# A hybrid conv / chunked-gMLP decoder layer on one core: first two steps reordered, conv taps moved to a two-way filter, output projection by halves

## The chip, the cores and the metric

One NeuronCore of one Trainium2 chip runs the whole program. The metric is the device time of one execution in microseconds (us); lower is better. TensorE (PE) multiplies, VectorE (DVE), ScalarE (ACT) and GpSimd (POOL) do the rest, SyncE (SP) issues most DMAs.

## The reference, cut to what matters

```python
def _layer(x, conv_buf, chunk_len, norm_g, w_in, conv_w, conv_b, ...):
    h = _rmsnorm(x, norm_g)
    z = h @ w_in                                    # 1024 -> 6144
    a_val, a_gl, a_gate, b_u, b_v, b_gate = jnp.split(z, ...)
    a_in = a_val * jax.nn.sigmoid(a_gl)
    a_seq = jnp.concatenate([conv_buf, a_in], axis=1)
    a_conv = _depthwise_conv_valid(a_seq, conv_w, conv_b)          # 31 taps
    a_out = silu(_layernorm(a_conv, a_ln_g, a_ln_b)) * silu(a_gate)
    vn = _layernorm(b_v, b_ln_g, b_ln_b)
    gated = _spatial_gate(vn in chunks of 128, w_s, b_s)
    b_out = b_u * gated * silu(b_gate)
    y = x + jnp.concatenate([a_out, b_out], axis=-1) @ w_out       # 2048 -> 1024
    return y, new_buf, b_v[:, -chunk_len:]
```

One layer, then a final RMSNorm. 1024 prompt positions and 8 sample positions are computed together (1032 columns), all in float32; channels lie on the 128 partitions.

## The kernel before, in words

**Products.** Every float32 factor is split into a high part h (rounded to fp32r by an ACT copy) and a low part l (DVE: factor minus h), and a product is three matmuls: h·H, l·H, h·L. The input projection is done by Strassen's scheme with 7 products: `PRODS` (line 37) names for each *slot* 0 to 6 of a *step* the weight piece, the form of x (nB11, nT3, T2, nB21, T1, nT4, nB22) and the PSUM bank. `prod` (261) issues 24 matmuls of 258 columns for one slot. A step computes two 128-channel blocks (a *unit*) for all 1032 columns; steps 0 and 1 are special, they compute units P0 and P1 together for the first half of the columns and then for the second half, since x is still being prepared. There are 24 steps (`steps`, 804): `P` units feed the conv, `v` the spatial gate's input, `B` its u and gate, `G` the conv branch's gate.

**Order.** The program is written out by hand, engine queues run in the order in which the code calls them. During steps 0 and 1 `start_x` (846) prepares the forms of x (`xform`, 229: a DVE difference, an ACT copy h, a DVE subtraction l) and the weights' sums and splits (`wsum` 150, `wsplit` 155), after the slot's matmuls. The RMS statistic of the second column half comes from four ACT squares and 96 small matmuls (`stat_q`, 198) in slots 2 and 3 of step 0. PSUM is moved on by ACT copies between banks (lines 944, 948, 952) and read out by `evac0` (ACT) and `evac1` (DVE).

**Fill.** Work without a fixed place stands in a queue `fill`, and `pump` (101) takes from it while the estimated DVE time is below the estimated PE time plus a margin. The conv of channel tile k (`conv_items`, 339) enters it when unit Pk is finished. 20 of its 31 taps are done in pairs on DVE: 10 pairs (`NF`, 337), each three multiply-adds of 512 columns (line 369), the first of them an ACT product. The other 11 taps are ACT products of 1024 columns (`prod`, 379 and 381) that are added up by accumulating DMAs issued from POOL (385), alternately into two buffers; two more accumulating DMAs add these to the result `c` (407), then `c` is added to a running sum `ssum` and stored (331 to 334). After tile 7 come mean, centring (444), squares, variance (`var`), and, once the steps are over, the normalisation `mixa_norm`, `mixa_gate`. All these share a pool of 51 buffers of 4 KB per partition (`U`, tag "u"), where a new tile waits until the buffer's last reader or writer is done.

**Output projection.** `ow` (657) has 48 passes: 3 column groups (384, 384, 264) x 2 halves of the 2048 inputs (the spatial half first, then the conv half) x 8 output tiles. Each pass loads and splits its weights anew (`load_w`, `split_w`) and issues 24 matmuls (`mmo`, 698); both halves of an output tile add up in PSUM. Within the first group's spatial half the layer norm's rest is pumped.

```python
    657	    ow = [(g, half, nt) for g in range(NG) for half in (1, 0) for nt in range(8)]
    382	                if n < 2:
    383	                    st["g", n] = p
    384	                else:
    385	                    G.dma_start(st["g", n % 2], p, accum_op=ALU.add)
    102	        while fill and est["dve"] < est["pe"] + margin:
```

Of the kernel before, what the change touches and what calls it, by code (L numbers as in the profile page):

```python
# [27 lines left out]
EPS = 1e-6  # L28
NU = 51
# [12 lines left out]
def body(ctx, tc, xT, w_in, w_out, state, stateT, conv_w, vecs, wsT, w00, b_s,  # L42
# [36 lines left out]
    cws = C([128, 8, 10], "cws")  # L79
# [75 lines left out]
    def wsplit(u, i):  # L155
        if i == 4:
            t = U([128, 2, 512], f"HL{u}_4", F32R)
            h, l, r = t[:, 0:1, :], t[:, 1:2, :], R[u, 4][:, 0:1, :]
        else:
            h = U([128, 2, 512], f"H{u}_{i}", F32R)  # L160
            l = U([128, 2, 512], f"L{u}_{i}", F32R)
            r = R[u, i]
        HL[u, i] = (h, l)
        A.activation(h, r, AF.Copy)  # L164
        V.tensor_tensor(out=l, in0=r, in1=h, op=ALU.subtract)  # L165
        dve(0.62 if i == 4 else 1.15)

# [22 lines left out]

    def stat_x(p, ps):
# [5 lines left out]

    def stat_q(p, q, ps):
        sq = xsq.pop((p, q))
        for t in range(2):  # L200
            for c in range(6):
                T.matmul(ps[:CN, 0, c:c + 1], lhsT=sq[:, t, c // 3, CN * (c % 3):CN * (c % 3) + CN], rhs=ones_m[:, :1],
                         start=q == 0 and t == 0 and c == 0, stop=q == 3 and t == 1, skip_group_check=True)
# [23 lines left out]
    raw = {}  # L227

    def xform(p, name):
# [3 lines left out]
        if name in ("nB11", "nB21", "nB22"):  # L233
            kh, a = {"nB11": (0, 0), "nB21": (1, 0), "nB22": (1, 1)}[name]
            for j in range(2):
                src = X[p, 2 * kh + j][:, :, a, :]
                hv = h[:, 2 * j:2 * j + 2, :]
                A.activation(hv, src, AF.Copy, scale=-1.0)
                V.scalar_tensor_tensor(out=l[:, 2 * j:2 * j + 2, :], in0=src, scalar=-1.0, in1=hv, op0=ALU.mult,  # L239
                                       op1=ALU.subtract)  # L240
            dve(1.3)
# [13 lines left out]
        V.tensor_tensor(out=l, in0=t, in1=h, op=ALU.subtract)  # L255
        dve(2.4)
# [80 lines left out]
    NF = 10  # L337

    def conv_items(k, ap):
# [26 lines left out]
        def taps(i):  # L366
            def f():
                for e in range(3):
                    V.scalar_tensor_tensor(out=st["m"][e], in0=src(e, i), scalar=wt(e, i), in1=st["m"][e],  # L369
                                           op0=ALU.mult, op1=ALU.add)  # L370
            return f

        def gtap(n):

            def f():
# [6 lines left out]
                if n < 2:  # L382
                    st["g", n] = p
# [736 lines left out]
```

## Time and profile before

| | |
|---|---|
| median of 3 runs | 870.5 us (869.26 to 873.74) |
| the profiled execution | 872.84 us, its span (first to last instruction) 871.1 us |
| PE busy | 777.8 us (89%), 5720 matmuls |
| DVE / ACT busy | 606.4 us (70%) / 435.9 us (50%) |
| mean granted TensorE clock | 0.941 of full speed (2.4 GHz) |

An engine's busy time counts overlapping instructions once. Matmuls are pipelined: one shows some 0.28 us, but in a full stream a new one starts every 0.12 us. "L" numbers are lines of the kernel.

### The profile page before, as it was taken

To read this page: it belongs to the slowest core of one execution; us is meant where nothing else is said; L and a number is where in the kernel's file an instruction comes from. 1 tells how busy PE (TensorE), PEld (TensorE's weight loads), DVE (VectorE), ACT (ScalarE), POOL (GpSimd) and SP (SyncE) were. 2 spreads that over 40 slices of the span, in tenths; PEclk is the share of its full clock that TensorE was granted. 3 is DMA by queue.
4 is the path that set the end of the run, shared out by engine and by line. 5 is a ranking of instruction groups with operands and counts; after the bars stand their busy time and mean duration, and the time that the engine had idled before them with its cause. 6 is when DMAs were issued, how large, how long until landed. Compare 5 with 4: busy or idle time off the path is not lost. (4 is left out here: it accounts for less than half of the span.)

```text
span 871.1 us, 14256 instructions
## 1 busy us (share of the span) xinstructions
PE 777.8 (89%) x5720; PEld 762.3 (88%) x5720; DVE 606.4 (70%) x860; ACT 435.9 (50%) x594; POOL 97.5 (11%) x119
## 2 busy tenths in 40 slices
PE   7797999798887879989799788899999889999995
PEld 6797999798887778989799788899999889999995
DVE  5648998695867568868788787698327756726843
ACT  4443465565545646457574665354336534414431
POOL 1010012121211211211112131000100000000000
PEclk8879999999997989989999899999999999999997
DMA  8031268797895797985979989572369544384461
GB/s 298 0 120 68 75 145 188 179 246 163 202 204 109 225 222 152 215 225 101 249 159 243 213 190 219 199 230 96 112 200 374 168 141 145 115 323 121 133 232 51
DMA packets 68091, 153.56 MB, mean 176 GB/s; under 512 B 7512, under 2 KB 28696, under 8 KB 68008
## 3 DMA queue, kind: packets, MB, share of 16 engines
q1 hardware_dynamic: 53624, 100.15, 33.6%
q0 software_dynamic: 14400, 52.49, 30.9%
q8 instruction: 45, 0.74, 0.4%
q14 instruction: 22, 0.18, 0.1%
HBM read 80.41 MB, written 24.38 MB: 120 GB/s over the span
## 5 line engine op out<-in xcount | busy, mean ns | idle before, releaser
L165 DVE TENSOR_TENSOR L<-R,H 128x1024 fp32r<-128x1024 f32 x72 | 87.9, 1222 | 81.8 <-ACT H L164 60.1
L704 PE MATMUL po<-mh,wh 128*128 128x384 f32 (+1 forms) x384 | 124.5, 324 | 3.9 <-ACT wh L670 3.9
L704 PE MATMUL po<-mh,wl 128*128 128x384 f32 (+1 forms) x384 | 124.3, 324 | 1.9 <-DVE wl L672 1.9
L704 PE MATMUL po<-ml,wh 128*128 128x384 f32 (+1 forms) x384 | 124.0, 323 | 0.2 <-DVE ml L695 0.2
L381 ACT ACTIVATE prod<-apad,cw 128x1024 f32<-128x1024 f32 x80 | 90.7, 1146 | 64.7 <-DMA prod<-prod 40.6
L269 PE MATMUL zb<-hT,H 128*128 128x258 f32 x384 | 84.8, 304 | 25.2 <-ACT zb L944 14.8
L369 DVE SCALAR_TENSOR_TENSOR m<-d,cw,m 128x512 f32<-128x512 f32 x144 | 101.5, 747 | 0.0
L385 POOL DMA_DIRECT2D prod<-prod x72 | 62.4, 866 | 308.5 <-ACT prod L381 198.8
L269 PE MATMUL zb<-hnB,HL 128*128 128x258 f32 x384 | 73.6, 308 | 23.6 <-DVE apad L303 15.7
L164 ACT ACTIVATE H<-R 128x1024 fp32r<-128x1024 f32 x72 | 75.4, 1050 | 34.1 <-DMA prod<-prod 11.9
L269 PEld LDWEIGHTS zb<-hT,H 128*128 128x128 f32 x384 | 64.2, 205 | 27.8 <-ACT zb L944 15.8
L269 PEld LDWEIGHTS zb<-hnB,HL 128*128 128x128 f32 x384 | 60.4, 210 | 26.4 <-DVE apad L303 16.9
L269 PE MATMUL zb<-lT,H 128*128 128x258 f32 x384 | 82.2, 298 | 0.7 <-DVE lT L255 0.7
L269 PE MATMUL zb<-hT,L 128*128 128x258 f32 x384 | 82.3, 297 | 0.0
L269 PE MATMUL za<-lnB,H 128*128 128x258 f32 x384 | 78.0, 285 | 1.4 <-DVE lnB L239 1.4
L269 PE MATMUL za<-hnB,H 128*128 128x258 f32 x384 | 78.3, 285 | 0.0
L269 PE MATMUL za<-hnB,L 128*128 128x258 f32 x384 | 77.9, 284 | 0.0
L704 PEld LDWEIGHTS po<-mh,wh 128*128 128x128 f32 x384 | 73.1, 190 | 4.5 <-ACT wh L670 4.5
L704 PEld LDWEIGHTS po<-mh,wl 128*128 128x128 f32 x384 | 73.3, 191 | 3.0 <-DVE wl L672 2.8
L704 PEld LDWEIGHTS po<-ml,wh 128*128 128x128 f32 x384 | 73.0, 190 | 0.5 <-DVE ml L695 0.5
L672 DVE TENSOR_TENSOR wl<-wr,wh 128x1024 fp32r<-128x1024 f32 x48 | 58.1, 1222 | 17.2 <-ACT wh L670 15.1
L269 PEld LDWEIGHTS zb<-lT,H 128*128 128x128 f32 x384 | 64.4, 205 | 1.0 <-DVE lT L255 1.0
(172 smaller groups left out, 1622.2 us busy)
## 6 DMA issues: line engine op xcount, KB each, us to landing
prod<-prod POOLq DMA_DIRECT2D x72, 512.0 KB, 6.2
R<-w_in SPq DMA_DIRECT2D x96, 256.0 KB, 5.8
wr<-w_out SPq DMA_DIRECT2D x48, 512.0 KB, 4.9
c<-prod POOLq DMA_DIRECT2D x14, 512.0 KB, 4.6
x<-xT SPq DMA_DIRECT2D x8, 516.0 KB, 6.0
mbD<-row SPq DMA_DIRECT2D x8, 516.0 KB, 3.8
vD<-va SPq DMA_DIRECT2D x8, 512.0 KB, 5.8
vh<-vD SPq DMA_DIRECT2D x8, 512.0 KB, 9.1
```

The source lines that it names most:

```text
L164: A.activation(h, r, AF.Copy)
L165: V.tensor_tensor(out=l, in0=r, in1=h, op=ALU.subtract)
L269: T.matmul(z[:, s, :PW], lhsT=HL[u, wi][we][:, wh, cs], rhs=F[name, p][xe][:, kt, :], start=first, stop=(kt == 3 and we == 1), skip_group_ ...
L369: V.scalar_tensor_tensor(out=st["m"][e], in0=src(e, i), scalar=wt(e, i), in1=st["m"][e], op0=ALU.mult, op1=ALU.add)
L381: A.activation(p, ap[:, j:j + NP_], AF.Copy, scale=cw[:, k, j:j + 1])
L385: G.dma_start(st["g", n % 2], p, accum_op=ALU.add)
L672: V.tensor_tensor(out=wl[s], in0=r, in1=wh[s], op=ALU.subtract)
L704: T.matmul(z, lhsT=w[:, cs], rhs=m_[g, half, kt][e], start=(half == 1 and kt == 0 and e == 0 and w is wh[s]), stop=(half == 0 and kt == KT ...
```

## The change

Three parts. (1) In steps 0 and 1 the two halves of `xform` are called apart (`xpre`: difference and h; `xpost`: l), `wsplit` likewise (`whigh`, `wlow`), and `start_x` runs ahead of a slot's matmuls and in a new order; the second half's squares come before the first step and are added up by three accumulating DMAs from POOL, so that 12 small matmuls (24 instructions, each float32 one counting twice) take the place of 96. (2) `NF` is 12: 24 taps go by pairs on DVE, 7 by ACT products, with one accumulating buffer instead of two; the three multiply-adds of a pair are pumped one by one. (3) The output projection does the spatial half for all columns first, 8 passes that are added to x in SBUF (`evac_h`), then the conv half by column groups with 8 weight tiles that stay: 16 splits instead of 48.

```diff
+NF = 12
-    cws = C([128, 8, 10], "cws")
+    cws = C([128, 8, NF], "cws")
...
+    def sum_x_dma(p):
+        for a, b in ((0, 1), (2, 3), (0, 2)):
+            G.dma_start(xsq[p, a], xsq.pop((p, b)), accum_op=ALU.add)
...
-    NF = 10
-
     def conv_items(k, ap):
...
-        def taps(i):
+        def taps(i, e):
             def f():
-                for e in range(3):
-                    V.scalar_tensor_tensor(out=st["m"][e], in0=src(e, i), scalar=wt(e, i), in1=st["m"][e],
-                                           op0=ALU.mult, op1=ALU.add)
+                V.scalar_tensor_tensor(out=st["m"][e], in0=src(e, i), scalar=wt(e, i), in1=st["m"][e],
+                                       op0=ALU.mult, op1=ALU.add)
             return f
...
-                if n < 2:
-                    st["g", n] = p
+                if n == 0:
+                    st["g"] = p
                 else:
-                    G.dma_start(st["g", n % 2], p, accum_op=ALU.add)
+                    G.dma_start(st["g"], p, accum_op=ALU.add)
...
-            while n * (NF - 1) < i * len(others):
+            while n < len(others) and n * (NF - 3) < i * len(others):
                 fill.append(("dve", 0.0, gtap(n)))
                 n += 1
-            fill.append(("dve", 2.0, taps(i)))
+            for e in range(3):
+                fill.append(("dve", 0.665, taps(i, e)))
...
-            for e in range(2):
-                g = st.pop(("g", e))
-                if k < 7:
-                    G.dma_start(c[:, :NP_], g, accum_op=ALU.add)
-                else:
-                    V.tensor_tensor(out=c[:, :NP_], in0=c[:, :NP_], in1=g, op=ALU.add)
+            g = st.pop("g")
+            if k < 7:
+                G.dma_start(c[:, :NP_], g, accum_op=ALU.add)
+            else:
+                V.tensor_tensor(out=c[:, :NP_], in0=c[:, :NP_], in1=g, op=ALU.add)
...
-    ow = [(g, half, nt) for g in range(NG) for half in (1, 0) for nt in range(8)]
+    ow = [(half, nt) for half in (1, 0) for nt in range(8)]
...
+    def evac_h(nt, z, c):
+
+        y = yt[nt]
+        if z is not None:
+            yy = y[:, :768].rearrange("p (a b) -> p a b", a=2)
+            V.tensor_tensor(out=yy, in0=z[:, :, :384], in1=yy, op=ALU.add)
+            dve(0.9)
+        else:
+            V.tensor_tensor(out=y[:, GS[2]], in0=c, in1=y[:, GS[2]], op=ALU.add)
+            dve(0.4)
...
+        for q in range(4):
+            square_x(1, q)
+        sum_x_dma(1)
...
         def start_x(si, slot):
 
             if si == 0:
                 if slot == 0:
-                    xform(0, "T2")
-                    for u in range(2):
-                        wsum(u, "S2")
-                        wsplit(u, 2)
+                    both(lambda u: wsum(u, "S2"), lambda u: whigh(u, 2))
+                    xpost(0, "T2")
+                    xpre(0, "nB21")
+                    both(lambda u: wlow(u, 2))
...
                 if slot == 4:
+                    ps = PS("e", "xst1")
+                    stat_x(1, ps)
+                    rstd_x(1, ps)
+                if slot == 5:
                     bcast_x(1, PS("e", "xbc1"))
...
+        for s in range(8):
+            nt = ow[s][1]
+            z = PS("ab"[nt % 2], f"pz{nt}")
...
+            for g in range(NG):
+                dst = z[:, g, :384] if g < 2 else zc[:, nt % 2, :264]
+                mmo(dst, s, g, range(0, 4))
+                if g == 0:
...
+                    split_w(s + 1)
+                pump(3.0 if nt < 7 else 1e9, nt < 7)
+                mmo(dst, s, g, range(4, 8))
...
+        for g in range(NG):
+            for nt in range(8):
+                s = 8 + nt
...
+                if g == 0:
+                    load_w(s + 2)
+                    split_w(s + 1)
```

What the order looks like on the engines that wait, at three places.

ACT's queue in step 0 before, from the copy for form T2 on (xsq are the second half's squares, H the weights' high parts, hnB, hT, hnT the forms' high parts; p and zc are copies out of PSUM):

```order
L254 ACTIVATE hT_0_303<-tT_0_305 128x1032
L164 ACTIVATE H_2_311<-R_2_147 128x1024
L164 ACTIVATE H_2_316<-R_2_149 128x1024
L948 ACTIVATE p_0_345<-ze_320 128x516
L183 ACTIVATE xsq_0_347<-x_0_151 128x1032
L183 ACTIVATE xsq_1_349<-x_1_153 128x1032
L238 ACTIVATE hnB_0_351<-x_2_130 128x516
L238 ACTIVATE hnB_0_351<-x_3_132 128x516
L183 ACTIVATE xsq_2_357<-x_2_155 128x1032
L183 ACTIVATE xsq_3_359<-x_3_157 128x1032
L952 ACTIVATE zc_386<-zb_301 128x2x258
```

And with the change:

```order
L190 ACTIVATE xsq_3_269<-x_3_157 128x1032
L255 ACTIVATE hnT_0_280<-tnT_0_282 128x1032
L255 ACTIVATE hT_0_286<-tT_0_288 128x1032
L164 ACTIVATE H_2_296<-R_2_147 128x1024
L164 ACTIVATE H_2_299<-R_2_149 128x1024
L242 ACTIVATE hnB_0_303<-x_2_130 128x516
L242 ACTIVATE hnB_0_303<-x_3_132 128x516
L973 ACTIVATE zb_333<-za_293 128x2x258
L255 ACTIVATE hT_0_338<-tT_0_340 128x1032
L164 ACTIVATE H_3_344<-R_3_143 128x1024
L164 ACTIVATE H_3_347<-R_3_145 128x1024
L977 ACTIVATE p_0_374<-ze_335 128x516
```

The squares have moved ahead of hnT; the PSUM copy zb, which slot 2 needs (before it stood ahead of hT), now stands behind both H_2 and hnB.

POOL's queue for conv tile 0, before (the accumulating DMAs of the products, named by tap, into two buffers, then both into c):

```order
L385 DMA prod0_0_976<-prod0_22_1083 128x1024
L385 DMA prod0_21_978<-prod0_23_1123 128x1024
L385 DMA prod0_0_976<-prod0_24_1160 128x1024
L385 DMA prod0_21_978<-prod0_25_1231 128x1024
L385 DMA prod0_0_976<-prod0_26_1234 128x1024
L385 DMA prod0_21_978<-prod0_27_1252 128x1024
L385 DMA prod0_0_976<-prod0_28_1283 128x1024
L385 DMA prod0_21_978<-prod0_29_1330 128x1024
L385 DMA prod0_0_976<-prod0_30_1427 128x1024
L407 DMA c0_1447<-prod0_0_976 128x1024
L407 DMA c0_1447<-prod0_21_978 128x1024
```

And with the change:

```order
L395 DMA prod0_0_937<-prod0_25_970 128x1024
L395 DMA prod0_0_937<-prod0_26_1103 128x1024
L395 DMA prod0_0_937<-prod0_27_1174 128x1024
L795 AFFINE_SELECT wst_787<-wst_787 128x1024
L395 DMA prod0_0_937<-prod0_28_1368 128x1024
L395 DMA prod0_0_937<-prod0_29_1388 128x1024
L395 DMA prod0_0_937<-prod0_30_1459 128x1024
L417 DMA c0_1722<-prod0_0_937 128x1024
```

Eleven DMAs have become seven, and each of the seven now follows its predecessor into or out of the same buffer.

DVE's queue at the end of the last step (23), before (L and HL are the weights' low parts, row is a PSUM read-out, ml the low part of the projection's spatial input, wl of its weights):

```order
L165 TENSOR_TENSOR L_2_6358<-R_2_6213,H_2_6357 128x1024
L165 TENSOR_TENSOR L_3_6415<-R_3_6150,H_3_6414 128x1024
L165 TENSOR_TENSOR HL_4_6458<-R_4_6148,HL_4_6458 128x512
L303 TENSOR_TENSOR row_23_6541<-zb_6411,p_23_6442 128x2x258
L695 TENSOR_TENSOR ml_6545<-mr_0_6444,mh_6544 128x768
L695 TENSOR_TENSOR ml_6549<-mr_1_6447,mh_6548 128x768
L672 TENSOR_TENSOR wl_6554<-wr_6487,wh_6552 128x1024
L303 TENSOR_TENSOR row_23_6541<-zc_6485,p_23_6442 128x2x258
L695 TENSOR_TENSOR ml_6583<-mr_2_6450,mh_6582 128x768
L695 TENSOR_TENSOR ml_6587<-mr_3_6453,mh_6586 128x768
```

And with the change (c7 is the conv result of tile 7, prod7_0 its accumulating buffer, lc a centred tile):

```order
L414 TENSOR_TENSOR c7_6259<-m01_7_5746,m2_7_5747 128x512
L419 TENSOR_TENSOR c7_6259<-c7_6259,prod7_0_5832 128x1024
L168 TENSOR_TENSOR L23_3_6266<-R23_3_5958,H23_3_6265 128x1024
L168 TENSOR_TENSOR HL23_4_6305<-R23_4_5956,HL23_4_6305 128x512
L339 TENSOR_TENSOR ssum_1940<-ssum_1940,c7_6259 128x1032
L682 TENSOR_TENSOR wl0_6375<-wr0_6299,wh0_6373 128x1024
L696 TENSOR_TENSOR ml10_6378<-mr0_6254,mh10_6377 128x1032
L454 TENSOR_TENSOR lc0_6402<-lc0_6402,lnmean_6393 128x1032
L316 TENSOR_TENSOR row1_23_6422<-zb23_6252,p7_23_6293 128x2x258
L696 TENSOR_TENSOR ml11_6426<-mr1_6256,mh11_6425 128x1032
L454 TENSOR_TENSOR lc1_6404<-lc1_6404,lnmean_6393 128x1032
L316 TENSOR_TENSOR row1_23_6422<-zc23_6333,p7_23_6293 128x2x258
```

The end of the conv, which before was over in step 18, now stands in the last step; mean and centring, done before in steps 19 to 21, straddle its end, and the variance follows inside the projection's spatial half.

## Rows read from the trace of the kernel before

**Rows 1.** Busy time by stage: stretch in us, its length, busy us (and instructions) of PE, PE's weight loads, DVE, ACT and POOL, mean granted clock, DMA share, GB/s. The stretches are: step 0; step 1; steps 2 to 18, where the conv runs; steps 19 to 23; the projection's group 0 and the start of group 1; the rest of the projection.

```profile
26.41:68.80 42.39, 37.44 (x279) 36.49 (x278) 23.74 (x33) 20.08 (x26) 3.41 (x2) 0.80 0.24 82
68.80:98.05 29.25, 23.24 (x173) 22.19 (x172) 23.80 (x36) 11.95 (x19) 0.00 (x0) 0.94 0.13 42
98.05:545.10 447.05, 391.75 (x3042) 384.73 (x3041) 345.95 (x524) 259.74 (x351) 85.68 (x102) 0.94 0.82 190
545.10:659.35 114.25, 110.20 (x901) 107.93 (x900) 70.33 (x81) 49.19 (x73) 2.54 (x2) 1.00 0.53 180
659.35:747.72 88.37, 81.21 (x446) 79.00 (x444) 59.47 (x66) 44.56 (x57) 0.00 (x0) 0.96 0.53 182
747.72:857.59 109.87, 109.84 (x753) 109.63 (x752) 62.61 (x91) 40.00 (x59) 2.07 (x2) 1.00 0.52 178
```

**Rows 2.** Timeline of ACT, the PSUM copy at the end of a step's slot 0 (start, duration, what): that of step 2, of step 19 (17 steps later) and of step 23.

```profile
100.93 0.58 ACT L944 ACTIVATE zb<-za 128x516 f32<-128x516 f32 x1 [2.28 <-PE za L269]
...
548.00 0.58 ACT L944 ACTIVATE zb<-za 128x516 f32<-128x516 f32 x1 [2.33 <-PE za L269]
...
642.24 0.58 ACT L944 ACTIVATE zb<-za 128x516 f32<-128x516 f32 x1 [2.31 <-PE za L269]
```

**Rows 3.** The chain of work that ended last, pieces in order of time (start, duration, what): six pair multiply-adds of the conv in a row on DVE; on PE the gate's matmuls of a B unit, the layer norm's sum for the mean, the one for the variance, and one undisturbed slot of 24 matmuls.

```profile
477.58 3.99 DVE m L369 x6
...
556.55 1.80 PE gp L603 x16
...
559.72 2.00 PE lnm L427 x4
...
611.36 1.80 PE lnv L470 x18
...
616.24 2.88 PE zb L269 x24
```

**Rows 4.** Who waited for whom in the whole span: total us, times, longest.

```profile
POOL prod L385 <- DMA prod<-prod: 80.0, 23, 8.3
...
DVE L L165 <- ACT H L164: 60.1, 32, 5.2
...
ACT prod L381 <- DMA prod<-prod: 40.6, 12, 10.2
...
PE zb L269 <- DVE apad L303: 15.7, 5, 5.7
...
PE zb L269 <- ACT zb L944: 14.8, 5, 5.2
...
DVE c L400 <- DMA prod<-prod: 10.5, 2, 5.7
```

**Rows 5.** Timeline of POOL, ACT and PE at one stall of PE (start, duration, what, idle time before it).

```profile
310.60 0.85 POOL L385 DMA_DIRECT2D prod<-prod  x1 [6.08 <-DMA prod<-prod]
...
314.43 1.15 ACT L381 ACTIVATE prod<-apad,cw 128x1024 f32<-128x1024 f32 x1 [10.15 <-DMA prod<-prod]
...
317.63 0.58 ACT L944 ACTIVATE zb<-za 128x516 f32<-128x516 f32 x1
...
318.26 0.80 PE L269 MATMUL zb<-hT,H 128*128 128x258 f32 x2 [5.16 <-ACT zb L944]
```

**Rows 6.** Timeline of PE in steps 0 and 1 (start, duration, what, idle time before it): the end of a wait for a weight's high part in slot 2 of step 0, the statistic's matmuls behind slots 2 and 3, and the wait at slot 1 of step 1.

```profile
37.90 0.58 PE L269 MATMUL zb<-hT,H 128*128 128x258 f32 x1 [2.56 <-ACT H L164]
...
43.41 4.03 PE L202 MATMUL xst<-ones_m,xsq 128*86 128x1 f32 x48
...
51.80 4.89 PE L202 MATMUL xst<-ones_m,xsq 128*86 128x1 f32 x48
...
61.50 1.47 PE L211 MATMUL xbc<-ident,xrs 86*128 86x86 f32 x12
...
76.17 0.51 PE L269 MATMUL ze<-hnT,H 128*128 128x258 f32 x2 [2.68 <-ACT hnT L254]
```

**Rows 7.** Groups of instructions by line (count | busy us, mean ns of one | idle time before them, and what ended it): the conv's ACT products, a weight's low part on DVE, its high part on ACT, the projection's weight split on DVE, the power for the statistic of x on POOL.

```profile
L381 ACT ACTIVATE prod<-apad,cw 128x1024 f32<-128x1024 f32 x80 | 90.7, 1146 | 64.7 <-DMA prod<-prod 40.6 <-DMA cD<-c 11.1 <-PE zb L269 7.5
...
L165 DVE TENSOR_TENSOR L<-R,H 128x1024 fp32r<-128x1024 f32 x72 | 87.9, 1222 | 81.8 <-ACT H L164 60.1 <-DMA prod<-prod 9.5 <-DMA c<-prod 7.4
...
L164 ACT ACTIVATE H<-R 128x1024 fp32r<-128x1024 f32 x72 | 75.4, 1050 | 34.1 <-DMA prod<-prod 11.9 <-issue 10.9 <-DVE R L152 5.7
...
L672 DVE TENSOR_TENSOR wl<-wr,wh 128x1024 fp32r<-128x1024 f32 x48 | 58.1, 1222 | 17.2 <-ACT wh L670 15.1 <-DMA yt<-xT 1.9
...
L207 POOL TENSOR_TENSOR xrs<-xrs,nhalf 86x6 f32<-86x6 f32 x2 | 4.0, 1986 | 53.8 <-DVE xrs L206 53.8
```

**Rows 8.** The instructions of line 385, POOL's accumulating DMAs of the products: ns on POOL (least, median, most), first and last start; then the us from issue to landing.

```profile
L385 POOL DMA_DIRECT2D prod<-prod x72: 834/853/1497, 115.8 to 538.8; - x72
...
DMA to landing us min/median/max: 4.4/6.2/11.3
```

**Rows 9.** DMA issues by line: the accumulating DMAs into c, count, KB each, median us to landing.

```profile
c<-prod POOLq DMA_DIRECT2D x14, 512.0 KB, 4.6
```

**Rows 10.** The chain inside the projection: the statistic's matmuls (ov) of group 0 and of group 1, each standing behind 39 matmuls of the following group, and the broadcast (ob) in between.

```profile
747.72 0.56 PE ov L732 x6
...
752.58 0.67 PE ob L741 x6
...
814.22 0.56 PE ov L732 x6
```

More of the change, by code (lines that the diff above doesn't have):

```diff
@@ L254, in xform, with xpost @@
         A.activation(h, t, AF.Copy)
-        V.tensor_tensor(out=l, in0=t, in1=h, op=ALU.subtract)
-        dve(2.4)
+        dve(1.21)
+    def xpost(p, name):
+        h, l = F[name, p]
+        if name in NEG:
+            kh, a = NEG[name]
+            for j in range(2):
+                V.scalar_tensor_tensor(out=l[:, 2 * j:2 * j + 2, :], in0=X[p, 2 * kh + j][:, :, a, :], scalar=-1.0,
+                                       in1=h[:, 2 * j:2 * j + 2, :], op0=ALU.mult, op1=ALU.subtract)
+            dve(1.22)
+            return
+        V.tensor_tensor(out=l, in0=raw[name], in1=h, op=ALU.subtract)
+        dve(1.15)
     Z = {}
@@ L838, in body, with both @@
         scale_x(0, 1)
-        xform(0, "nB11")
+        xpre(0, "nB11")
+        for q in range(4):
+            square_x(1, q)
+        sum_x_dma(1)
+        xpost(0, "nB11")
         scale_x(0, 2)
         scale_x(0, 3)
-        xform(0, "nT3")
-        xst = []
+        xpre(0, "nT3")
+        xpre(0, "T2")
+        xpost(0, "nT3")
+        def both(*fns):
+            for f in fns:
+                for u in range(2):
+                    f(u)
         def start_x(si, slot):
@@ L858, in start_x @@
[L858 to L874 removed]
+                    xpost(0, "nB21")
@@ L908, in body @@
                     Z[bank] = PS(bank, f"z{bank}{si}")
+                if si < 2:
+                    start_x(si, slot)
                 if si and own and slot == 1:
@@ L1015, in body @@
         opened.append(True)
+        for kt in (6, 7):
+            prep_m(1, kt)
+        zc = None
+        pend = []
+        for s in range(8):
+            nt = ow[s][1]
+            z = PS("ab"[nt % 2], f"pz{nt}")
+            if nt % 2 == 0:
+                zc = PS("c", f"pzc{nt}")
+            load_w(s + 2)
+            load_y(nt + 2) if nt < 6 else None
+            for g in range(NG):
+                dst = z[:, g, :384] if g < 2 else zc[:, nt % 2, :264]
+                mmo(dst, s, g, range(0, 4))
+                if g == 0:
+                    if s:
+                        wh.pop(s - 1)
+                        wl.pop(s - 1)
+                    for x in pend:
+                        evac_h(*x)
+                    pend = []
+                    split_w(s + 1)
+                pump(3.0 if nt < 7 else 1e9, nt < 7)
+                mmo(dst, s, g, range(4, 8))
+                pump(3.0 if nt < 7 else 1e9, nt < 7)
+                while outq:
+                    slot_end()
+            pend = [(nt, z, None)]
+            if nt % 2:
+                pend += [(nt - 1, None, zc[:, 0, :264]), (nt, None, zc[:, 1, :264])]
+        hend = pend
         pend = []
@@ L1048, in body @@
                 if g > 0 and nt == 1:
[L1049 removed]
+                    stat_o(g - 1, "a")
                 if g > 0 and nt == 2:
[L1051 removed]
+                    bcast_o(g - 1, "a")
                 if g > 0 and 3 <= nt < 6:
                     norm_o(g - 1, range(3 * nt - 9, min(3 * nt - 6, 8)))
[L1054 to L1065 removed]
@@ L1066, in body @@
-            if half == 1 and g == 0:
-                pump(8.0, nt < 6)
-            mmo(s, range(5, 8))
-            if half == 0 and nt % 2:
-                pend = [(g, nt - 1), (g, nt)]
+                mmo(po[g, nt], s, g, range(5, 8))
+                if nt % 2:
+                    pend = [(g, nt - 1), (g, nt)]
         for x in pend:
             evac_o(*x)
-        stat_o(2, "a")
-        bcast_o(2, "b")
+        stat_o(2, "b")
+        bcast_o(2, "c")
         norm_o(2, range(8))
```

247 lines of the change are left out of this document (102 added, 145 removed).

## The prediction, made before the changed kernel was run

> **What bounds the kernel now.** I read the table by stage first. PE is busy nearly everywhere, so a share of busy time says little; what counts is how far each stage is from an undisturbed stream of matmuls. One undisturbed slot of 24 matmuls takes 2.88 us [rows 3], a step of seven slots 20.2 us.
>
> Steps 2 to 18 take 548.00 - 100.93 = 447.1 us [rows 2]. Seventeen clean steps are 342.7 us; six B units with 1.8 us for the gate and some 0.4 for its sample part (13), four v units with transposes (11) and the causal sums (2) make 369. So 78 us are lost here, 4.6 us a step. Steps 19 to 22 take 94.2 us [rows 2] for 80.6 of slots, two gates (4.4), lnm with its sample part (2.4) and lnv (1.8) [rows 3]: 5 us lost. The loss is where the conv runs, and there no engine is full: DVE 346 and ACT 260 of 447 us, the DMA engines 0.82, the granted clock 0.94 [rows 1].
>
> The list of waits and one stall show the mechanism. PE waits for a PSUM copy or an evacuation on ACT or DVE [rows 4]; ACT comes late to it because it stood in front of a conv product whose buffer an accumulating DMA still held: 10.15 us of idle time, then product, evacuation, PSUM copy, and PE starts 5.2 us late [rows 5]. In sum ACT stood 40.6 us before products for such DMAs, DVE 60.1 us for ACT's high parts [rows 4]. What PE loses is the waits plus the matmuls at the lower clock behind them: in step 0 the slot between 37.90 and 43.41 us took 5.5 us instead of 2.88 behind waits [rows 6].
>
> Steps 0 and 1 take 71.6 us [rows 1] for 14 x 2.88 = 40.3 us of slots. The projection's matmuls of 384 columns run at (814.22 - 747.72 - 0.56 - 0.67) / 384 = 0.170 us [rows 10]; the first 423 should take 71.9 and two broadcasts about 2 (the gate's row as an estimate, [rows 3]), but the stage takes 88.4 [rows 1]: 14.5 us lost. The rest of the projection loses nothing.
>
> **The change part by part.**
>
> *Steps 0 and 1.* The 96 statistic matmuls cost 4.03 + 4.89 us [rows 6], and DVE and PE stood behind them; 12 remain, about 1.1 us, and the broadcast's 1.5 [rows 6] stays. The squares run on ACT while it waits for DVE, and their DMAs need at least two landings in a row, 2 x (0.85 + 4.4 to 6.2) = 10.5 to 14 us [rows 8], over by slot 4. I walk the new queues with 1.05 us per ACT high part, 1.22 per DVE low part, 1.99 for POOL's power [rows 7], and take as estimates: slot 2 waits 2.0 us (zb behind hT, two H and two hnB on ACT); slot 4 waits 1.8 (its two H and the copy zc); the broadcast in slot 5 waits 2.7, since DVE reaches the statistic only behind both HL_4 and POOL's power follows; slot 1 of step 1 waits 2.9 for hnT and lnT, as it waits 2.7 for hnT now [rows 6]. With 4 us for slots at the lower clock: 40.3 + 1.1 + 1.5 + 9.4 + 4 = 56.3. I take **-15 us**; without any wait it would be -28, with only the statistic gone -7.
>
> *Conv.* Out go 32 ACT products (1.15 us each, 37 us) and, per tile, 3 accumulating DMAs of products and one into c: 31 of 86 in all. In come 48 multiply-adds at 3.99 / 6 = 0.665 us [rows 3], 32 us of DVE. They lie beside PE as long as DVE keeps up: DVE's 346 + 70 us of steps 2 to 23 [rows 1] become 416 + 32, less 17 for centring and squares' sums that move into the projection, plus 5 for the sample state's sums that move in from step 1: about 436 against a clean PE time of 476 (22 x 20.2 and the extras above but for lnv). It hides, with little air. Since `pump` stops at the same estimated DVE load, the conv stretches: a tile takes about 2.6 steps instead of 2.1 and runs through steps 2 to 22. Per step there are (48 + 7 + 14) / 21 = 3.3 POOL DMAs instead of 100 / 17 = 5.9.
>
> How much of the loss per step stays? If each DMA does the same harm, 4.6 x 3.3 / 5.9 = 2.6 us. A lone accumulating DMA lands in 4.6 us [rows 9], against 6.2 where two chains overlap [rows 8]: 2.6 x 4.6 / 6.2 = 1.9. I take 2.0, nearest to that row, with 0.8 (DMA waits nearly gone) and 4.6 (as now, since DVE has less air) as ends. Steps 2 to 22 then take 369 + 89.2 - 1.8 (lnv leaves) + 21 x 2.0 = 498 instead of 541: **-43 us**, from -68 to +12.
>
> The landing time is also what one page prices otherwise. By the Trainium skill, "DMA: Bandwidth & Descriptors", section "Anatomy of one DMA — SWDGE (gpsimd) path", such a DMA takes about 2.0 us plus bytes over 436 GB/s, an estimate of 3.2 us for 512 KB. The trace disagrees: 4.4 at least for an accumulating one [rows 8]. By the page's price the loss would be 1.3 us a step and the sum 14 us lower.
>
> *End of the steps.* Tile 7 now ends in step 23: DVE must wait there for the last of the serial accumulations before it adds them to c7, and the low parts of slots 4 and 6 queue behind it; the same wait cost up to 5.7 us once before [rows 4]. Eight low parts of 1032 columns (1.22 us) stand in place of four of 768 before the projection. I take **+4 us**, 0 to +9.
>
> *Projection.* 32 splits go (1.22 DVE and 1.05 ACT each [rows 7]); they lay beside PE, so nothing for themselves. What they free is group 0: it no longer needs the normalised conv half after 192 matmuls but after 576, some 88 us, in which DVE has 66 us to do: 24 x 1.22 for the normalisation, 16 for centring, 10 for splits and some 11 for `evac_h`. So 14.5 us of loss become lnv's 1.8 [rows 3] and about 3 of waits (for lnv behind DVE, and at its power): **-9.5 us**, from -13 to -3. The tail stays.
>
> **Sum.** Against the span of 871.1: 871.1 - 15 - 43 + 4 - 9.5 = 807.6. The profiled execution is 1.7 us longer than its span and 2.3 above the median of the runs, so a run takes the span less 0.6: **807 us**.
>
> **Rivals.**
>
> *Waits nearly gone* (0.8 us a step): 871.1 - 15 - 68 + 4 - 9.5 = 782.6, a run of 782. For it: 31 DMAs and 37 us of ACT less, finer pumping. Against it: buffers are still freed by DMAs issued just before. 13%.
>
> *DVE becomes the bound.* DVE's idle time in steps 2 to 18 is 447 - 346 = 101 us, 5.9 a step, most of it waits for ACT [rows 1, 4]. If the same 5.9 a step stays and DVE is the chain, steps 2 to 23 take 436 + 22 x 5.9 = 566 us instead of 561: 871.1 - 15 + 5 + 4 - 9.5 = 856, a run of 855. The Trainium skill, "Perfetto Trace Analysis", section "Optimizing Scalar/DVE Operations", speaks for this one: where DVE is saturated, work should go from it to ScalarE, and this change goes the other way. The rows speak half against it, since ACT's waits are for the DMAs that the change removes. 22%.
>
> *One accumulator's chain paces the conv* (the slower side). In a tile six accumulations d follow each other, then one into c (0.85 + 4.6) and two more issues: 6 d + 7.7 us for a tile, eight tiles and 10 us to start. ACT's products wait for the buffers, and PE for ACT. At the rows' 0.85 + 6.2 = 7.05 it is 50 us a tile, inside the forecast's 62 (2.6 steps of 498 / 21 us); from d = 10.3 the kernel is 0.5% slower than before, and at 11 it takes 908 us. Only the longest landing, 11.3 [rows 8], lies there, and fewer DMAs compete. 3%.
>
> *No net change* (865 to 876, from several terms at their bad ends): 4%.
>
> **How the numbers follow.** Forecast 58%, its own range 785 to 832. What a measurement of this kernel can tell from no change is about 0.5%, 866 to 875. The forecast and the first two rivals lie below it: faster 0.93, same 0.04, slower 0.03. The range reaches from the forecast's side into both faster rivals: 782 to 843.
>
> **What would show it.** Right: step 1 begins near 53 to 56 us and step 2 near 82; the copies at the end of slot 0 of steps 2 and 23 lie about 498 us apart; ACT's waits for accumulating DMAs fall to a third, DVE is over 85% busy there; the conv half of the projection starts without a wait. Wrong: the 498 stays above 530 with DVE saturated (second rival), or POOL waits for its own DMAs all through (third); or PE stands at lnv or lnb for more than 5 us in the projection.

## The result, and the profile after

The changed kernel takes 822.2 us (median of 4 runs, 821.5 to 825.9) against 872.1 us of the kernel before in the same session: ratio 0.944, 95% interval 0.940 to 0.948. The prediction was 807 us, in a range of 782 to 843. The profiled execution has a span of 821.0 us against 871.1.

First the stages. ACT's PSUM copy at the end of a step's slot 0 in steps 2, 22 and 23 of the changed kernel (start, duration, what), which answers to [rows 2]:

```profile
81.03 0.58 ACT L973 ACTIVATE zb<-za 128x516 f32<-128x516 f32 x1 [2.28 <-PE za L282]
...
549.39 0.58 ACT L973 ACTIVATE zb<-za 128x516 f32<-128x516 f32 x1 [1.43 <-PE za L282]
...
576.75 0.58 ACT L973 ACTIVATE zb<-za 128x516 f32<-128x516 f32 x1 [2.70 <-PE za L282]
```

Busy time by stage of the changed kernel (columns as in [rows 1]): steps 2 to 22, from copy to copy; from step 23's copy to the projection's first matmul; the spatial half; the conv half:

```profile
81.03:576.75 495.72, 464.31 (x3751) 458.14 (x3750) 416.65 (x617) 259.85 (x370) 60.69 (x72) 0.98 0.62 155
...
576.75:604.80 28.05, 21.89 (x150) 20.38 (x149) 13.09 (x15) 10.46 (x14) 0.00 (x0) 0.88 0.86 324
604.80:713.00 108.20, 98.54 (x613) 95.76 (x613) 68.78 (x67) 42.18 (x43) 2.31 (x2) 0.98 0.45 159
713.00:808.00 95.00, 93.81 (x602) 93.14 (x600) 38.39 (x68) 15.48 (x27) 1.70 (x2) 1.00 0.14 53
```

| stretch | before | after | change | predicted |
|---|---|---|---|---|
| start to the copy of step 2 | 100.93 | 81.03 | -19.9 | -15 |
| steps 2 to 22 | 541.3 | 495.7 | -45.6 | -43 |
| copy of step 23 to the projection | 17.1 | 28.05 | +10.9 | +4 |
| projection, first to last matmul | 198.2 | 203.2 | +5.0 | -9.5 |
| tail | 13.5 | 13.0 | -0.5 | 0 |
| span | 871.1 | 821.0 | -50.1 | -63.5 |

The gain is where it was forecast, and 7.5 us larger (65.5 against 58). At the end 15.9 us were lost where the forecast had a gain of 5.5, so the last two stages came out 21 us worse than forecast. From 81.03 to 576.75 the granted clock is 0.98 (before 0.94 and 1.00 in the two parts of it, [rows 1]), the DMA share 0.62, DVE 417 of 496 us, 84%. The list of waits (total us, times, longest) answers to [rows 4]:

```profile
POOL prod L395 <- DMA prod<-prod: 118.5, 21, 8.2
...
DVE L L168 <- ACT H L164: 36.1, 26, 4.5
...
ACT prod L391 <- DMA prod<-prod: 24.7, 4, 7.7
...
PE zb L282 <- DVE row L316: 12.2, 5, 5.0
...
PE zb L282 <- ACT zb L973: 8.8, 4, 5.6
...
PE zb L282 <- DVE apad L316: 4.8, 3, 2.4
```

The read-outs `apad` and `row` are one line of code; the prediction's rows show only the first of them, the other stood before at

```profile
PE zb L269 <- DVE row L303: 7.8, 6, 1.9
```

POOL now waits longer for its own DMAs, since one chain has taken the place of two. ACT's wait before products falls from 40.6 to 24.7 us and DVE's for high parts from 60.1 to 36.1; PE's wait for the PSUM copy falls from 14.8 to 8.8 us, and its wait for the read-out `apad` from 15.7 to 4.8. Only PE's wait for the read-out `row` has grown, from 7.8 to 12.2 us, and 8.9 of these lie in steps 22 and 23. Most of the loss is made at two places. First step 23, DVE's timeline (start, duration, what, idle time before it):

```profile
578.58 1.23 DVE L419 TENSOR_TENSOR c<-c,prod 128x1024 f32<-128x1024 f32 x1
...
581.46 1.23 DVE L339 TENSOR_TENSOR ssum<-ssum,c 128x1032 f32<-128x1032 f32 x1
586.94 1.23 DVE L682 TENSOR_TENSOR wl<-wr,wh 128x1024 fp32r<-128x1024 f32 x1 [4.26 <-ACT wh L680]
588.09 1.23 DVE L696 TENSOR_TENSOR ml<-mr,mh 128x1032 fp32r<-128x1032 f32 x1
597.58 1.23 DVE L454 TENSOR_TENSOR lc<-lc,lnmean 128x1032 f32<-128x1032 f32 x1 [8.27 <-DMA lc<-cD]
598.73 0.69 DVE L316 TENSOR_TENSOR row<-zb,p 128x516 f32<-128x516 f32 x1
```

The centring of the first tile waits 8.27 us for its reload from DRAM, which SP issued at 586.67, behind the eight loads of the spatial half. The read-out that PE needs for slot 6 stands right behind it. Then the spatial half's seventh pass (a pass is the 72 matmuls of one output tile): on DVE the last two normalised tiles, and behind them the read-outs, the last two of which empty PSUM bank c, where two output tiles share the last column group:

```profile
688.49 1.22 DVE L529 TENSOR_TENSOR lc<-lc,row 128x1032 f32<-128x1032 f32 x1
690.84 1.23 DVE L696 TENSOR_TENSOR ml<-lc,mh 128x1032 fp32r<-128x1032 f32 x1 [1.13 <-ACT mh L695]
692.00 1.23 DVE L529 TENSOR_TENSOR c<-c,row 128x1032 f32<-128x1032 f32 x1
694.41 1.23 DVE L696 TENSOR_TENSOR ml<-c,mh 128x1032 fp32r<-128x1032 f32 x1 [1.19 <-ACT mh L695]
695.56 0.95 DVE L718 TENSOR_TENSOR yt<-pz,yt 128x768 f32<-128x768 f32 x1
696.43 0.76 DVE L721 TENSOR_TENSOR yt<-pzc,yt 128x264 f32<-128x264 f32 x2
```

PE at both places and at the start of the spatial half (start, duration, what, idle time before it):

```profile
599.47 0.80 PE L282 MATMUL zb<-hnB,HL 128*128 128x258 f32 x2 [5.05 <-DVE row L316]
...
607.70 0.44 PE L704 MATMUL pz<-ml,wh 128*128 128x384 f32 x1 [0.82 <-DVE ml L696]
...
609.98 0.44 PE L704 MATMUL pz<-ml,wh 128*128 128x384 f32 x1 [1.21 <-DVE ml L696]
...
697.24 0.59 PE L704 MATMUL pzc<-mh,wh 128*128 128x264 f32 x1 [5.03 <-DVE yt L721]
```

The first pass took 16.2 us (604.80 to 620.97) and the seventh 18.5 (683.20 to 701.66), where an undisturbed one takes 11.3.

Steps 0 and 1, PE's waits over 0.6 us and the statistic, which answer to [rows 6]:

```profile
33.88 0.51 PE L282 MATMUL zb<-hT,H 128*128 128x258 f32 x2 [0.95 <-ACT zb L973]
...
40.22 2.00 PE L206 MATMUL xst<-ones_m,xsq 128*86 128x1 f32 x24 [0.32 <-ACT p L977]
...
46.44 1.57 PE L215 MATMUL xbc<-ident,xrs 86*128 86x86 f32 x12 [1.23 <-POOL xrs L211]
...
59.48 0.52 PE L282 MATMUL ze<-hnT,H 128*128 128x258 f32 x2 [1.27 <-ACT hnT L255]
...
60.74 0.51 PE L282 MATMUL ze<-lnT,H 128*128 128x258 f32 x2 [0.75 <-DVE lnT L268]
```

### The profile page after: what moved, and what is told of

The parts are those of the page before. It is cut to its first block, busy times and chain, and to the rows that moved or that the text cites. A ratio compares the mean times of both kernels' runs of the same rounds, so it can differ in the third digit from the quotient of the medians.

```text
span 821.0 us, 13810 instructions
## 1 busy us (share of the span) xinstructions
PE 752.5 (92%) x5648; PEld 738.4 (90%) x5648; DVE 606.0 (74%) x871; ACT 370.6 (45%) x510; POOL 72.6 (9%) x91
## 5 line engine op out<-in xcount | busy, mean ns | idle before, releaser
L379 DVE SCALAR_TENSOR_TENSOR m<-d,cw,m 128x512 f32<-128x512 f32 x176 | 128.3, 752 | 0.0
L168 DVE TENSOR_TENSOR L<-R,H 128x1024 fp32r<-128x1024 f32 x72 | 87.7, 1220 | 54.0 <-ACT H L164 36.1
L282 PE MATMUL zb<-hnB,HL 128*128 128x258 f32 x384 | 71.3, 300 | 17.1 <-DVE row L316 12.2
L391 ACT ACTIVATE prod<-apad,cw 128x1024 f32<-128x1024 f32 x48 | 54.8, 1145 | 39.9 <-DMA prod<-prod 24.7
L395 POOL DMA_DIRECT2D prod<-prod x48 | 41.5, 865 | 338.8 <-ACT prod L391 166.3
L379 DVE SCALAR_TENSOR_TENSOR m<-apad,cws,m 128x512 f32<-128x512 f32 x88 | 65.4, 744 | 0.0
L704 PE MATMUL po<-mh,wl 128*128 128x384 f32 (+1 forms) x192 | 61.6, 321 | 1.2 <-DVE wl L682 1.2
L704 PE MATMUL po<-mh,wh 128*128 128x384 f32 (+1 forms) x192 | 61.7, 321 | 0.0
L704 PE MATMUL po<-ml,wh 128*128 128x384 f32 (+1 forms) x192 | 61.4, 320 | 0.0
L282 PEld LDWEIGHTS zb<-hT,L 128*128 128x128 f32 x384 | 60.8, 194 | 0.0
L282 PEld LDWEIGHTS za<-hnB,H 128*128 128x128 f32 x384 | 59.8, 191 | 0.0
L282 PEld LDWEIGHTS za<-lnB,H 128*128 128x128 f32 x384 | 59.8, 191 | 0.0
## 6 DMA issues: line engine op xcount, KB each, us to landing
mr<-mbD SPq DMA_DIRECT2D x8, 516.0 KB, 11.3
```

Of the source, the lines that this page charges most:

```text
L168: V.tensor_tensor(out=l, in0=R[u, i][:, 0:1, :] if i == 4 else R[u, i], in1=h, op=ALU.subtract)
L282: T.matmul(z[:, s, :PW], lhsT=HL[u, wi][we][:, wh, cs], rhs=F[name, p][xe][:, kt, :], start=first, stop=(kt == 3 and we == 1), skip_group_ ...
L391: A.activation(p, ap[:, j:j + NP_], AF.Copy, scale=cw[:, k, j:j + 1])
L395: G.dma_start(st["g"], p, accum_op=ALU.add)
L704: T.matmul(z, lhsT=w[:, cs], rhs=m_[half, kt][e][:, GS[g]], start=(kt == 0 and e == 0 and w is wh[s]), stop=(kt == KT - 1 and w is wl[s]), ...
```

## The experiments

Ratios are to the kernel before, with 95% intervals; stage times are of the profiled execution. Three kernels below that run the same program up to step 22 (`lc_early`, `low_later`, `both_mend`) took 498.5, 492.5 and 497.6 us for steps 2 to 22 in it, so a difference of up to 6 us in that stage shows nothing.

**The parts by themselves.** Each takes only its own pieces of the change, on the kernel before.

```diff
 p1_steps01:
+        sum_x_dma(1)
...
+                if si < 2:
+                    start_x(si, slot)
 p2_conv24:
-    NF = 10
+NF = 12
...
+                for e in range(3):
+                    fill.append(("dve", 0.665, taps(i, e)))
 p3_halves:
-    ow = [(g, half, nt) for g in range(NG) for half in (1, 0) for nt in range(8)]
+    ow = [(half, nt) for half in (1, 0) for nt in range(8)]
```

> Part 1 alone (new order of forms and weights in steps 0 and 1) on the kernel before. In the changed kernel steps 0 and 1 became 19.9 us shorter (copy of step 2 at 81.03 instead of 100.93). Theory A (the parts stand for themselves): the same 20 us are gone here and nothing gives them back, time near 851, copy of step 2 near 81, copies of steps 2 and 23 still 541 us apart. Theory B (the conv's chain is what paces the middle, so an earlier start only shifts the waits): the copies lie 548 or more apart and the time is 858 to 868.

Measured: 0.981 (0.976 to 0.985), 856.8 us. The copy of step 2 comes at 81.01, as in the changed kernel, and the copies of steps 2 and 23 lie 546.8 us apart, not 541.3. In time 16.6 us of the 20 are kept, with an interval of 13 to 21, between the two theories' ranges. The 5.5 us that steps 2 to 22 take longer lie within the spread above, so this run does not decide between them.

> Part 2 alone (24 taps by the two-way filter, one accumulating buffer, single multiply-adds pumped) on the kernel before; its projection still needs the normalised conv half after the first 192 matmuls. Theory A (part 2 saves in steps 2 to 22 and its late end costs where the projection is not by halves): copies of steps 2 and 23 about 496 apart instead of 541, then the stretch from the last step's copy to the end of the projection's first group at least 20 us longer than before (11 in the last step, and PE standing 10 to 30 us for the layer norm), time 845 to 860. Theory B (the parts add up without touching each other): time near 826, no wait of PE over 5 us in the first group.

Measured: 0.963 (0.959 to 0.966), 839.7 us, below A's range. Steps 2 to 22 took 488.2 us, and from the projection's first matmul to the end it took 231.0 instead of 211.8. PE stood 18.5 us at one place for a weight's high part in the first group (the list of waits in that stretch):

```profile
PE po L702 <- ACT wh L668: 20.2, 2, 18.5
```

So A's mechanism holds, 19 us of it. A's sum was too high, because the stretch behind step 23's copy took only 19.5 us here, not 28, and because steps 2 to 22 took 8 us less than A had.

> Part 3 alone (projection by halves) on the kernel before; the conv ends in step 18 as before, so mean, centring and variance are over before the projection. Theory A (the term of the prediction was right for the projection itself, and what ate it in the changed kernel is the conv's late end): 14.5 us of loss in the first group become about 5, time near 861, spatial half from its first to its last matmul 95 to 97 us instead of 108. Theory B (the halves themselves bring nothing: normalisation, gate and split go back and forth between DVE and ACT and hold up the read-outs as in the changed kernel): time 866 to 872, PE waits some 5 us for a read-out in the spatial half here too.

Measured: 0.998 (0.995 to 1.000), 869.3 us. No difference that this measurement shows: B in time, though not in the size of its wait. Its spatial half took 100.5 us, more than A's 97: the first pass waits for high and low parts in a row as in the changed kernel (2.7 us in all), and PE waits 1.7 us for a read-out of bank c instead of 5.0. Without the other parts, the gain that the prediction had for this one is not there.

**Parts 1 and 2 without 3.**

```diff
-    ow = [(half, nt) for half in (1, 0) for nt in range(8)]
+    ow = [(g, half, nt) for g in range(NG) for half in (1, 0) for nt in range(8)]
```

> Parts 1 and 2 without part 3 (the projection as before). Part 2 alone showed PE waiting 18.5 us for a weight's high part in the first group, behind the normalisation on ACT and DVE. Theory A (that wait stays, and part 3 takes it away and brings 13 us of its own waits): 81 us to step 2, 496 to step 23, 19.5 and 231 from there, span 827, time 826 to 830; part 3 is worth 5 to 8 us here against 2 by itself. Theory B (the parts add up as measured alone, 871.2 less 16.6 and 32.5): time 822, part 3 is worth nothing.

Measured: 0.955 (0.952 to 0.958), 830.9 us: A, just above its range. PE's timeline has the wait:

```profile
667.52 0.69 PE L714 MATMUL po<-mh,wh 128*128 128x384 f32 x1 [17.07 <-ACT wh L680]
```

Against 0.944 part 3 is worth 0.011 (0.006 to 0.016), some 10 us, once part 2 has pushed the conv's end back; without it, the 2 us of `p3_halves` are not told from none.

**What in part 2 makes the gain.** Three kernels. `two_acc` has two accumulating buffers again, `nf10` 20 taps with one buffer, `nf10_two` both.

```diff
 two_acc, nf10_two:
-                if n == 0:
-                    st["g"] = p
+                if n < 2:
+                    st["g", n] = p
                 else:
-                    G.dma_start(st["g"], p, accum_op=ALU.add)
+                    G.dma_start(st["g", n % 2], p, accum_op=ALU.add)
 nf10, nf10_two:
-NF = 12
+NF = 10
```

> The changed kernel with two accumulating buffers used in turn, as before: per tile five accumulating DMAs of products and two into c instead of six and one, so the same seven, but in two chains that may overlap. Theory A (what counts is how many such DMAs there are and how much DVE and ACT wait for their buffers, not whether one chain is serial): within 3 us of the changed kernel's 822. Theory B (a lone chain lands faster, 4.6 us against 6.2, and this is part of the gain): slower by 5 to 12 us, median landing back at 6 us or more against the changed kernel's. Theory C (the serial chain holds buffers and so costs): faster by 4 or more.

Measured: 0.942 (0.938 to 0.946), 820.9 us: A. The median landing rose from 5.4 to 5.9 us, and the time did not move. ACT waits for accumulating DMAs before products hardly less than in the changed kernel, 22.5 us instead of 24.7; half of it is now for the DMAs into c:

```profile
ACT prod L391 <- DMA prod<-prod: 11.3, 4, 6.5
ACT prod L391 <- DMA c<-prod: 11.2, 3, 5.5
```

> The changed kernel with 20 taps by the two-way filter as before, 11 by ACT products (so 10 accumulating DMAs of products and one into c per tile, 11 instead of 7, and 32 ACT products more), but with the one accumulating buffer and the multiply-adds pumped one by one as in the change. Theory A (it is the number of products and their DMAs that costs): steps 2 to 22 take 530 to 545 us again, time 855 to 866. Theory B (the finer pumping and the buffers given back earlier make most of the gain): steps 2 to 22 below 515, time 842 or less. Theory C, the slower rival of the prediction (one chain of ten DMAs paces a tile): a tile takes over 10 x 7 us, steps 2 to 22 above 550, time over 875.

Measured: 1.083 (1.079 to 1.088), 941.4 us, steps 2 to 22 632 us: C, the slower rival of the prediction, at 20 taps. POOL's timeline of one tile:

```profile
331.51 0.89 POOL L395 DMA_DIRECT2D prod<-prod  x1 [4.80 <-issue]
336.71 0.87 POOL L395 DMA_DIRECT2D prod<-prod  x1 [4.32 <-DMA prod<-prod]
341.81 0.86 POOL L395 DMA_DIRECT2D prod<-prod  x1 [4.22 <-DMA prod<-prod]
346.99 0.86 POOL L395 DMA_DIRECT2D prod<-prod  x1 [4.32 <-DMA prod<-prod]
```

A link, from one DMA's issue to the next, takes 5.0 to 5.3 us at best, and a tile of ten links 62 to 78 (its DMA into c stands at 236.59, 314.74 and 376.48), against 61 us that the changed kernel has for one (from its first product's DMA at 91.8 to c7 at 579.8, over 8). ACT waits 93.6 us before products, PE 52.9 us for the PSUM copy in steps 2 to 22. The DMAs land faster than before (4.8 us in the median), so the landing time is not what counts, but how many stand in a row.

> The changed kernel with 20 taps by the two-way filter and two accumulating buffers, so part 2 of the change is undone but for the multiply-adds that are pumped one by one and the products that come a little earlier in a tile. With one buffer and 20 taps the kernel took 941 us, steps 2 to 22 632 us; with two buffers and 24 taps 821, as with one. Theory A (with 11 products a single buffer is one chain of ten transfers after each other, and that alone made 941; with two buffers the number of products and DMAs is what is left): steps 2 to 22 take 535 to 550 us, time 853 to 866, and the 24 taps are worth 35 to 45 us. Theory B (finer pumping is a good part of part 2's gain): steps 2 to 22 below 520, time below 845. Theory C (products that come earlier hold buffers and are what made 941): time over 880 here too.

Measured: 0.994 (0.991 to 0.997), 866.9 us, steps 2 to 22 558.9 us:

```profile
82.61:641.48 558.87, 490.12 (x3775) 476.87 (x3774) 408.28 (x592) 303.03 (x412) 90.03 (x105) 0.94 0.74 181
```

Both lie above A's ranges; B and C fall. Against `two_acc`, which has two buffers as well, the 24 taps are worth 0.052, some 45 us. Against `nf10` the second buffer is worth some 75 us: with ten links the lone chain costs that, and with six (`two_acc`) nothing that shows. Parts 1 and 3 alone gave 16.6 and 2.0 us; here only 5 are left, and steps 2 to 22 take 12 us longer than in `p1_steps01`. The two differ there by the single pumping and the earlier products, which would then cost some 12 us at 20 taps; no run separates them.

> The changed kernel without the accumulating DMAs of the products: left out is the adding up of six of the seven ACT products of a tile (they are computed and not used). DVE's and ACT's work stays the same. Steps 2 to 22 take 495.7 us in the changed kernel, some 454 of which are clean matmul time, so 2.0 us are lost a step. Theory A (the loss that is left comes from these DMAs holding buffers and competing): it falls to 0.8 us a step or less, steps 2 to 22 take 465 to 472, time 795 to 800. Theory B (what is left comes from the order of work on DVE and ACT, and the clock after it): steps 2 to 22 above 485, time 812 or more.

```diff
                 if n == 0:
                     st["g"] = p
-                else:
-                    G.dma_start(st["g"], p, accum_op=ALU.add)
```

Measured: 0.914 (0.911 to 0.918), 794.8 us; the stretch from copy to copy:

```profile
82.73:552.33 469.60, 457.22 (x3751) 453.09 (x3750) 412.74 (x613) 259.08 (x369) 18.01 (x23) 0.99 0.37 113
```

A. (469.6 - 454) / 21 = 0.7 us a step are lost with the same work on DVE and ACT, so 1.2 of the 2.0 come from the accumulating DMAs. The same DVE work, now 88% of the stretch, fits into 26 us less, so DVE did not bound the changed kernel. Whether these DMAs cost by the buffers that they hold or by what they load on the DMA engines (a share of 0.37 instead of 0.62) is not separated.

**The end.** `lc_early` issues the reload at the start of step 23, `low_later` takes a normalised tile's low part on DVE one tile later (`mixa_gate` ends with ACT's high part, `low_m` is the subtraction), `both_mend` does both. `ln["load"]` is the reload that stood in `mean`.

```diff
 lc_early:
+                    if slot == 0:
+                        for kt in range(2):
+                            ln["load"](kt)
                     if slot < 4:
                         load_m(2 * slot)
 low_later:
                 fill.append(("dve", 1.15, lambda k=k - 1: mixa_gate(k)))
+            if k > 1:
+                fill.append(("dve", 1.15, lambda k=k - 2: low_m(k)))
```

> The changed kernel, where the reload of the first two stored conv tiles for the centring is issued at the start of step 23, ahead of the loads for the projection's spatial half, and no longer behind the mean. In the changed kernel DVE stood 8.27 us for this reload with a PSUM read-out queued behind it, PE waited 5.05 us for that read-out, and the slot behind it took 5.3 instead of 2.88 us. Theory A (this wait is what made the last step 10.9 us longer): the wait is gone, the stretch from step 23's copy to the projection's first matmul falls from 28 to 20 or 21 us, and time to 813 to 815 (ratio to before 0.933 to 0.936). Theory B (the loads of that step all share full DMA queues, so another load is late instead): the stretch stays above 25 us, time 819 to 822.

Measured: 0.941 (0.939 to 0.944), 817.9 us. In the trace A: the 5.05 us wait is gone and the stretch from step 23's copy to the projection is 20.4 us; the wait of 5.0 us for bank c stays. In time it is above A's range, and the 2.3 us against the changed kernel lie within both intervals.

> The changed kernel, where the low part of a normalised tile is taken on DVE one tile later, behind the next tile's work, so that DVE no longer stands some 1.19 us per tile for ACT's high part. In the changed kernel DVE took 44 us for the eight tiles, the read-out of bank c came behind them, and PE waited 5.03 us for it in the seventh pass of the spatial half, with 13 matmuls at the lower clock after it. Theory A (DVE's back and forth with ACT makes the read-out late): the eight tiles take 34 to 36 us, the wait is under 1 us, time about 816 (ratio 0.935 to 0.938). Theory B (the read-out is late because the queue is filled by an estimate that knows nothing of DVE's delay, whatever the order): a wait over 3 us stays, time 820 to 823.

Measured: 0.940 (0.937 to 0.942), 816.3 us, as A had it, though the 0.004 against the changed kernel lie within both intervals; the trace decides. DVE does the eight tiles in 34.7 us instead of 44.1, without a wait for ACT's high part, and PE no longer waits at bank c:

```profile
682.45 1.23 DVE L533 TENSOR_TENSOR c<-c,row 128x1032 f32<-128x1032 f32 x1
683.59 1.23 DVE L708 TENSOR_TENSOR ml<-lc,mh 128x1032 fp32r<-128x1032 f32 x1
684.81 1.23 DVE L708 TENSOR_TENSOR ml<-c,mh 128x1032 fp32r<-128x1032 f32 x1
685.96 0.95 DVE L729 TENSOR_TENSOR yt<-pz,yt 128x768 f32<-128x768 f32 x1
686.83 0.76 DVE L732 TENSOR_TENSOR yt<-pzc,yt 128x264 f32<-128x264 f32 x2
```

> Both edits at once: the earlier reload and the later low parts. Theory A (two separate waits): the gains add up to 12 to 14 us, time 808 to 811 (ratio 0.927 to 0.931), which is about the predicted 807. Theory B (one chain: an earlier start of the normalisation moves the same wait to another place): no more than the larger one of the two gains, 814 to 816.

Measured: 0.931 (0.928 to 0.934), 808.9 us: A. Against the changed kernel 0.013 (0.008 to 0.018), 12 us, which is clear of the noise where either edit alone was not. The stretch behind step 23's copy takes 20.4 us, the spatial half 102.8 and the projection from its first to its last matmul 198, as before the change. It is the fastest version with the whole computation.

> Both mends (earlier reload, later low parts) and the spatial half prepared earlier: its eight loads are issued in slots 0 and 1 of step 23 instead of 0 to 3, its splits stand in slots 3 to 6 (two, two, three, one) instead of reaching behind the last slot, and the loads of x for the read-outs follow the last step. In the kernel with both mends the first pass of the spatial half takes some 5 us more than its matmuls, waiting for high and low parts in a row (0.73, 0.82, 1.21 us and smaller ones). Theory A (these waits come from the place of the splits in the queues): the first 48 matmuls of 384 columns take 8.5 to 9.5 us instead of 13, time 804 to 806 (ratio 0.925 to 0.928). Theory B (the loads are limited by the DMA queues and a split ahead of a read-out waits for its load and holds the read-out up): PE waits over 2 us in slots 5 or 6 of the last step, time 808 to 814.

```diff
-                    if slot >= 3:
-                        prep_m(1, slot - 3)
-                    if slot > 4:
-                        prep_m(1, slot - 1)
+                    for kt in {3: (0, 1), 4: (2, 3), 5: (4, 5, 6), 6: (7,)}.get(slot, ()):
+                        prep_m(1, kt)
```

Measured: 0.935 (0.932 to 0.938), 812.7 us, no better than both mends (0.931). The waits of the first pass are gone, as A said, but neither theory had what came instead: the splits that stand earlier raise the estimate by which the fill is pumped, so the mean slides into the projection, its copy stands behind four splits and a weight's on ACT, and PE waits there:

```profile
605.66 0.60 PE L442 MATMUL lnms<-ssum,ones_m 128*128 128x8 f32 x2 [4.49 <-ACT lnmean L440]
```

## Why the prediction was right, and where a term was not

The sum, 807 against 822, came out within the range in part by luck, since its errors have opposite signs: steps 0 to 22 gained 7.5 us more than forecast, the end of the steps and the projection lost 21 us against it. Of the signs given for being right, steps 1 and 2 began about as stated, the copies lay 496 us apart and the conv half of the projection starts without a wait. Two others failed: ACT's wait before products fell to 0.61 and not to a third, and DVE was 84% busy, not over 85%.

*Conv, -43 against -45.6.* Right, and the size too: taking the mean's 2.4 us out as well (it went to step 23), 454 us are clean and 41.7 / 21 = 2.0 us a step are lost, as forecast. That the products and their DMAs cost is shown by `nf10_two` against `two_acc` (45 us) and, for the DMAs alone, by `no_acc` (26 us more); that they do it by holding buffers and ACT is argued from the waits. The factor 4.6 / 6.2 from the landing time was not a reason: `two_acc` and `nf10` change the landing and the time does not follow. Without this factor the prediction's sum gives 2.6 us a step and -30 us, so the exact 2.0 was luck. DVE as the bound, with 22% the largest rival, fell: DVE rose to 84%, and `no_acc` does the same work at 88% in 26 us less. The Trainium skill, "Perfetto Trace Analysis", section "Optimizing Scalar/DVE Operations", says that offloading some work from a saturated DVE to ScalarE may make sense; in `no_acc` DVE is 88% busy and the stretch still comes within 16 us of its clean 454, and no run shows from where on DVE would be saturated.

*One chain.* The mechanism of the 3% rival exists: with ten links it paced the kernel (`nf10`). With six it cost nothing that shows: at d = 5.2 to 5.3 us, six links and 7.7 us are 39 of the 61 us of a tile. Between six and ten nothing was run.

*Landing price.* By the Trainium skill, "DMA: Bandwidth & Descriptors", section "Anatomy of one DMA — SWDGE (gpsimd) path", an estimate of 3.2 us; no accumulating DMA of products here landed under 4.4 in the changed kernel or in `nf10`. The measurement decides.

*Steps 0 and 1, -15 against -19.9.* Right, mis-sized: PE's waits are 4.5 us (the rows above) where 9.4 were walked out, and 51.0 us from the first slot (26.93) to step 2 (77.88) where 56.3 were forecast. Slot 4 does not wait at all. One term was miscounted: the rows count instructions, 96 for 48 small matmuls, and 12 matmuls of 24 instructions remain, so the 8.92 us become 2.2 and not 1.1; the row shows 2.00. What the order and what the smaller statistic gave was not run apart. Step 1 begins at 55.17, inside the 53 to 56 of the prediction, step 2 at 77.88 instead of 82.

*End of the steps, +4 against +10.9.* A wait at that place was forecast, but another: not c7 for the last accumulation (DVE goes through without a wait at 578.58) but the centring for its reload, 5.05 us of PE and 2.4 for the slot behind it at the lower clock (599.47 to 604.80 for 24 matmuls, 5.3 instead of 2.88). 3.4 us are the mean itself, most of which the sum had left in steps 2 to 22.

*Projection, -9.5 against +5.* This term failed in three ways. The clean rate of 0.170 us was taken over a stretch in which 39 of the 384 matmuls have 264 columns; a stream of 384 columns alone runs at 0.174 (sum over 33 matmuls, 621.14 to 626.88), so before only 88.4 - 423 x 0.174 - 2, some 13 us, were lost, not 14.5. The first pass waits for splits of the spatial half where group 0 did not need so many (2.7 us behind low parts, here and in `p3_halves`). And DVE's 66 us were counted as work without the 1.19 us per tile in which DVE stands for ACT: 44 us for eight tiles, so that PE waited 5 us for bank c's read-out (`low_later`). With the lower clock behind these waits, the first and the seventh pass lost 12 us together, where the sum had some 3 us of waits in the whole stage. Repairing the reload and this order gives 808.9 us, near the predicted 807, but not by the predicted terms: the projection then still takes 198 us, where the sum had 188.7.

## What to carry to other kernels

Work that is taken off a busy stage ends later, and its end meets whatever was placed there; walk the queue of the engine that reads out PSUM past that point, with the loads it waits for. Where two engines hand one tile back and forth, count the round trip and not the busy times, and put the next tile's work between. Accumulating transfers into one buffer are a chain: set their number, times the 5.2 us that one took here, against the time that the tile has.

## What the runs showed of the hardware

An accumulating transfer of 512 KB never landed in under 4.4 us in any run, and one behind another into the same buffer took 5.0 to 5.3 us a link where nothing else held it (`nf10`). After a stream at full clock and a wait of 5 us the granted clock was lower: behind 697.24 the 264-column matmuls started every 0.22 us instead of 0.12 up to 700 us, at a mean granted clock of 0.50 (the 1.2 GHz level); from 697 to 703 it is 0.72.
